# Cross attention: moving the query products and the logits from four PSUM banks to two

## The chip, the cores and the metric

One core of a Trainium2 chip runs the whole program in one launch. The metric is the device time of that launch in microseconds, as the median of several runs; lower is better. PSUM, the memory that matmuls write, has eight banks of 128 x 512 float32 each, and this program hands them out by name: two to a pool called `mm`, four to `ps`, two to `pr`.

## The reference

The program computes two transformer blocks in float32. The first holds a mixer of four branches, a dense feed-forward and a mixture of experts, over two layers. The second holds, in each of two layers, a mixer (an attention mixer in layer 0, gated linear attention in layer 1), a cross attention to 256 memory rows and a feed-forward. Only the cross attention of the second block is touched. With S = 256 tokens, a width of 1024 and 4 heads of 256:

```python
def mem_cross_attention(h, mem_n, w_q, w_kv, q_gain, k_gain, w_out):
    q = rmsnorm((h @ w_q).reshape(Bn, S, X_HEADS, X_HEAD_DIM), q_gain)
    k, v = jnp.split(mem_n @ w_kv, 2, axis=-1)
    k = rmsnorm(k.reshape(Bn, M, X_HEADS, X_HEAD_DIM), k_gain)
    s = jnp.einsum('bqhd,bkhd->bhqk', q, k) * (X_HEAD_DIM ** -0.5)
    p = jax.nn.softmax(s, axis=-1)
    o = jnp.einsum('bhqk,bkhd->bqhd', p, v).reshape(Bn, S, D_MODEL)
    return o @ w_out
```

## The kernel before

Weights come from HBM in chunks of 128 x 1024 float32 (512 KB). `load` (L536) issues the transfer on SyncE's queue, ScalarE copies the chunk to a rounded high part (`wh`, L469) and VectorE subtracts that to give the low part (`wl`, L482). A product with a weight is then three matmuls for each 128 rows of the weight: high by high, low by high and high by low (`lin`, L571). Six pairs of `wh` and `wl` buffers go round; a pair is free for the next chunk when the second of the two token tiles has used it.

A framework sets the order of the instructions on each engine when the program is built: it goes through the recorded operations with a list scheduler that knows priorities, data and buffers, and afterwards each engine runs its own list in that order and waits on semaphores. So a buffer that is free later can move an instruction to another place in the list of any engine. `bank` (L363) is where a PSUM tile is taken: a pool with n buffers gives the same bank again after n tiles, and the new tile waits until the old one has been read.

The cross attention (L1801) works so:

- `rms_split` (L1419) makes the normalized input X as a high and a low part, transposed.
- The query product is four groups of 24 matmuls of 128 x 512, called q0 to q3 here: q0 and q1 are the two token tiles of the first half of the columns (heads 0 and 1), q2 and q3 those of the second half (heads 2 and 3). `lin_tm` (L592) takes one bank for each, from `ps` (the argument on L1809).
- Each group is read by `head_rms` (L1744): ScalarE squares it (two ACTIVATE of 128 x 256 with a sum), VectorE makes the reciprocal root from the sums in a chain of small operations, and two SCALAR_TENSOR_TENSOR (L479, 128 x 256 each) scale the group and its gain into SBUF. That is the last reading of the bank. `to_fm` (L1770) turns the result with four transposes (L385, bank `pr`) and ScalarE copies it out.
- The logits are four groups, L0 to L3, one for a pair of heads and a token tile (hp, t on L1816 and L1817); each is four matmuls of 128 x 256 in one bank of `ps` (L1819), and each of these matmuls shows as two records, float32 being passed twice. L0 needs q0, L1 needs q1, L2 q2 and L3 q3.
- `softmax_pair` (L764) reduces the maximum on VectorE (TENSOR_REDUCE, L768), takes the exponential on ScalarE with its sum (the last reading of the bank), and scales on VectorE. `pT` (L790) turns the result (four transposes, P0 to P3 here, bank `pr`), ScalarE copies it out, and eight matmuls of 128 x 128 (o0 to o3, sixteen records each, bank `pr`) give the output, which `split` (L493) stores in parts.
- `out_proj` (L628) multiplies by the output weight in four accumulators of 128 x 512, all from `ps`, and `residual` (L1365) adds them to x.

Ahead of the cross attention stands the output projection of the mixer, with its four accumulators in `ps` too. The `mm` banks were last used by the projections of the mixer.

Of the kernel before, what the change touches and what calls it, by code (L numbers as in the profile page):

```python
# [21 lines left out]
S = 256  # L22
# [242 lines left out]
class Net:  # L265
# [27 lines left out]
    def T(self, shape, name=None, dt=F32, keep=False):  # L293

        n = 1
        for d in shape[1:]:
            n *= d
        w = n if dt != BF else (n + 1) // 2
        arena = self.arenar if dt == F32R else (self.cur or self.arena)
        ap, key = arena.alloc(w)  # L300
        key = (arena, key)
        own = self.scopes[-1] if self.scopes and not keep else None
        if own is not None:
            own.append(key)
        v = ap[:shape[0], :w]
        if dt not in (F32, F32R):
            v = v.bitcast(dt)
        if len(shape) == 3:
            v = v.rearrange("p (a b) -> p a b", a=shape[1])
        elif len(shape) == 4:  # L310
            v = v.rearrange("p (a b c) -> p a b c", a=shape[1], b=shape[2])
        self.keys[id(v)] = (key, v, own)
        return v
# [1487 lines left out]
    def cross_attention(self, x, l, kv, st, st2):  # L1801
        T = self.T
        kT, vm = kv
        with self.scope():
            g = self.rows(f"xg{l}", 0, 256)
            X, rs = self.rms_split(x, f"norm_mem_q{l}", st)
            qT = T([128, 8, S])
            for b in range(2):
                for t, _, ps in self.lin_tm(X, f"xq{l}", b, ("ps", "ps")):  # L1809
                    with self.scope():  # L1810
                        qn = T([128, 512])
                        self.head_rms(qn, ps, 2, 256, g, rs[t])
                        self.to_fm(qT, t, qn, 4 * b)
            self.free(*X, *rs)
            O = self.newX()
            for hp in range(2):  # L1816
                for t in range(2):  # L1817
                    with self.scope():
                        lg = self.ps([128, 2, S])  # L1819
                        for j in range(2):  # L1820
                            h = 2 * hp + j
                            for k in range(2):
                                self.mmul(lg[:, j], qT[:, 2 * h + k, t * 128:(t + 1) * 128], kT[:, 2 * h + k, :], k == 0,
                                          k == 1)
                        P = self.softmax_pair(lg, S, 0.0625)
                        PT = self.pT(P, S, "pr")
                        o = self.pr([128, 4, 128])
                        for j in range(2):
                            h = 2 * hp + j
                            for m in range(2):  # L1830
                                for k in range(2):
                                    c = h * 256 + m * 128
                                    self.mmul(o[:, 2 * j + m], vm[k][:, c:c + 128], PT[:, 2 * j + k], k == 0, k == 1)
                        sl = (slice(None), slice(4 * hp, 4 * hp + 4), slice(t * 128, (t + 1) * 128))
                        self.split(O[0][sl], O[1][sl], o)
        self.free(kT, *vm)
        for t, b, ps in self.out_proj(O, f"xo{l}"):
            self.residual(x, t, b, ps, st2)
        self.free(*O)
# [304 lines left out]
```

## Time and profile before

| what | us |
| --- | --- |
| median of 3 runs | 2115.01 |
| lowest and highest run | 2112.03, 2117.79 |
| the profiled execution's own time | 2118.59 |
| span of the profile (first to last instruction) | 2116.9 |
| TensorE matmul (PE) busy | 2051.8 (97%) |
| VectorE (DVE) busy | 1495.5 (71%) |
| ScalarE (ACT) busy | 1153.3 (54%) |
| mean granted TensorE clock | 0.989 of full speed |

The times of single instructions come from the profiled execution, which is one run and not the median. The cross attention of layer 0 stands at about 1417 to 1481 us of the span, that of layer 1 at about 1854 to 1918 us. A row of the timeline gives the start, the length from the first start to the last end of a merged group, the engine, the line, the operation and, in brackets, the idle time before it and what ended it.

### The profile page before, as it was taken

What the parts mean: (1) busy time and instruction counts of PE and PEld (TensorE: products, weight loads), DVE (VectorE), ACT (ScalarE), POOL (GpSimd) and SP (SyncE); (2) the same over time, 40 slices, a digit from 0 to 9 for tenths busy, and PEclk for the clock granted to TensorE, in tenths of its full rate; (3) what the DMA queues carried; (4) which work ended last, traced back from release to release, by engine and by line L of the source; (5) the groups of instructions that cost most, each with busy time, mean ns of one, the idle gap of its engine ahead of it and who ended that gap; (6) DMA issues with size and microseconds to landing.
All of it is one profiled execution on the core that took longest, in us unless ns stands there. A gap on an engine that the chain in (4) does not pass through costs nothing. (4 is left out here: it accounts for less than half of the span.)

```text
span 2116.9 us, 31337 instructions
## 1 busy us (share of the span) xinstructions
PE 2051.8 (97%) x11520; PEld 1688.7 (80%) x11520; DVE 1495.5 (71%) x2916; ACT 1153.3 (54%) x1732; POOL 41.4 (2%) x111
## 2 busy tenths in 40 slices
PE   8999989997999999999999998999999999999999
PEld 8878778886986877888888886877888777878887
DVE  6876686546787578988888898976654657676453
ACT  5544544443544454777777785564544455555442
POOL 1000000000000000000000000000000000000000
PEclk9999999998999999999999999999999999999999
DMA  7333656551453455799999985545555353555551
GB/s 240 132 114 111 223 172 197 184 187 68 165 155 98 121 205 170 273 329 329 341 348 330 328 320 193 186 132 192 187 180 184 111 178 118 187 181 172 176 198 60
DMA packets 118259, 411.39 MB, mean 194 GB/s; under 512 B 13584, under 2 KB 13744, under 8 KB 118096
## 3 DMA queue, kind: packets, MB, share of 16 engines
q1 hardware_dynamic: 113184, 392.91, 54.3%
q0 software_dynamic: 4912, 16.39, 2.5%
q8 instruction: 92, 1.51, 0.3%
q14 instruction: 71, 0.58, 0.1%
HBM read 408.20 MB, written 1.05 MB: 193 GB/s over the span
## 5 line engine op out<-in xcount | busy, mean ns | idle before, releaser
L382 PE MATMUL mm<-wh,ar 128*128 128x512 f32 (+3 forms) x3200 | 976.2, 386 | 13.2 <-PEq L1714 4.4
L382 PEld LDWEIGHTS mm<-wh,ar 128*128 128x128 f32 x3200 | 588.3, 190 | 128.7 <-issue 14.2
L482 DVE TENSOR_TENSOR wl<-raw,wh 128x1024 fp32r<-128x1024 f32 (+3 forms) x464 | 548.1, 1193 | 197.0 <-ACT wh L469 186.0
L469 ACT ACTIVATE wh<-raw 128x1024 fp32r<-128x1024 f32 (+3 forms) x464 | 476.3, 1035 | 293.0 <-PE mm L382 173.1
L382 PE MATMUL mm<-wl,ar 128*128 128x512 f32 (+3 forms) x1600 | 613.4, 384 | 1.2 <-DVE wl L482 1.2
L482 DVE TENSOR_TENSOR wl<-af,wh 128x1024 fp32r<-128x1024 f32 (+2 forms) x300 | 347.3, 1173 | 152.3 <-ACT wh L469 138.5
L469 ACT ACTIVATE wh<-af 128x1024 fp32r<-128x1024 f32 (+2 forms) x300 | 303.7, 1020 | 155.6 <-PE mm L382 56.0
L382 PE MATMUL ps<-wh,ar 128*128 128x512 f32 x1104 | 349.2, 394 | 2.2 <-ACT ar L469 2.2
L382 PEld LDWEIGHTS mm<-wl,ar 128*128 128x128 f32 x1600 | 303.2, 189 | 56.3 <-DVE wl L482 2.4
L382 PEld LDWEIGHTS ps<-wh,ar 128*128 128x128 f32 x1104 | 206.2, 188 | 44.7 <-ACT ar L469 3.8
L382 PE MATMUL ps<-wl,ar 128*128 128x512 f32 x552 | 215.4, 390 | 0.0
L382 PE MATMUL mm<-ar,wh 128*128 128x256 f32 x704 | 131.8, 288 | 0.0
L469 ACT ACTIVATE ar<-pr 128x512 fp32r<-128x512 f32 (+1 forms) x124 | 67.0, 549 | 114.1 <-PE pr L385 97.9
L385 PE MATMUL pr<-ident,af 128*128 128x128 f32 x584 | 98.0, 287 | 31.4 <-DVE af L479 19.2
L382 PEld LDWEIGHTS ps<-wl,ar 128*128 128x128 f32 x552 | 103.7, 188 | 20.9
L385 PEld LDWEIGHTS pr<-ident,af 128*128 128x128 f32 x584 | 68.5, 144 | 63.6 <-issue 27.4
L382 PE MATMUL pr<-wh,ar 128*128 128x512 f32 x352 | 111.5, 394 | 1.2 <-ACT ar L469 1.0
L382 PEld LDWEIGHTS mm<-ar,wh 128*128 128x128 f32 x704 | 109.6, 191 | 3.3 <-issue 2.0
L469 ACT ACTIVATE af<-af 128x512 f32<-128x512 f32 (+5 forms) x132 | 63.8, 491 | 66.6 <-DVE af L482 48.4
L382 PE MATMUL mm<-ar,wl 128*128 128x256 f32 x352 | 99.4, 282 | 0.0
L482 DVE TENSOR_TENSOR ar<-pr,ar 128x512 fp32r<-128x512 f32 (+1 forms) x116 | 71.8, 628 | 37.2 <-ACT ar L469 37.1
L382 PE MATMUL pr<-af,af 64*64 64x32 f32 (+8 forms) x1132 | 84.4, 244 | 2.3 <-ACT af L469 2.3
(197 smaller groups left out, 1683.0 us busy)
## 6 DMA issues: line engine op xcount, KB each, us to landing
af<-in_e_dram SPq DMA_DIRECT2D x127, 512.0 KB, 5.2
raw<-in_win_dram SPq DMA_DIRECT2D x108, 512.0 KB, 4.6
raw<-in_e_dram SPq DMA_DIRECT2D x81, 512.0 KB, 5.2
af<-in_gu_dram SPq DMA_DIRECT2D x56, 512.0 KB, 4.2
af<-in_w_dram SPq DMA_DIRECT2D x42, 512.0 KB, 4.3
raw<-in_xkv_dram SPq DMA_DIRECT2D x32, 512.0 KB, 4.4
raw<-in_gu_dram SPq DMA_DIRECT2D x32, 512.0 KB, 4.5
af<-in_e_dram SPq DMA_DIRECT2D x38, 384.0 KB, 4.9
```

What stands on the lines that cost most here:

```text
L382: return self.pe(self.nc.tensor.matmul(out, lhsT=lhsT, rhs=rhs, start=start, stop=stop, skip_group_check=True), lhsT, rhs)
L385: return self.pe(self.nc.tensor.transpose(out, in_, ident), in_, ident, 1)
L469: return self.nc.scalar.activation(out, in_, f, **kw)
L482: return (eng or self.nc.vector).tensor_tensor(out, a, b, op=op)
```

## The change

The query products take their banks from `lin_tm`'s default, which is `mm` for both token tiles, and the logits take theirs from `mm`. So q0 to q3 and L0 to L3 go through two banks in turn, where they went through four. The output projection keeps its four banks of `ps`, and nothing else in the cross attention is in `ps` any more. No instruction is added or removed.

```diff
@@ cross_attention
-                for t, _, ps in self.lin_tm(X, f"xq{l}", b, ("ps", "ps")):
+                for t, _, ps in self.lin_tm(X, f"xq{l}", b):
...
-                        lg = self.ps([128, 2, S])
+                        lg = self.mm([128, 2, S])
```

The lists of the engines change with it, in both layers in the same way. Three places in layer 0 follow. In the names, `ps_15020` or `mm_15020` is the bank of q1, `15081` of q2, `15130` of q3, `15179`, `15208`, `15237` and `15266` of L0 to L3; `pr_15014`, `pr_15063`, `pr_15124` and `pr_15173` are the transposes of q0 to q3, and `pr_15191` those of P0.

TensorE at the end of q1, before:

```order
L382 MATMUL ps_15020<-wl4_85,ar2_76 128x512
L382 MATMUL ps_15081<-wh0_80,ar2_76 128x512
L382 MATMUL ps_15081<-wh0_80,ar3_77 128x512
...
L385 MATMUL pr_15014<-ident_93,af6_67 128x128 x2
L382 MATMUL ps_15081<-wh0_80,ar2_76 128x512
L385 MATMUL pr_15014<-ident_93,af6_67 128x128 x2
L382 MATMUL ps_15081<-wh0_80,ar3_77 128x512
```

and with the change:

```order
L382 MATMUL mm_15020<-wl4_85,ar2_76 128x512
L385 MATMUL pr_15014<-ident_93,af6_67 128x128 x4
L382 MATMUL mm_15081<-wh0_80,ar2_76 128x512
L382 MATMUL mm_15081<-wh0_80,ar3_77 128x512
...
L385 MATMUL pr_15063<-ident_93,af7_68 128x128 x2
L382 MATMUL mm_15081<-wl2_83,ar2_76 128x512
L385 MATMUL pr_15063<-ident_93,af7_68 128x128 x2
```

Twelve matmuls of q2 stood ahead of the transposes of q0; now none does. q2 takes the bank of q0, and 11 matmuls of q2 stand ahead of the transposes of q1, which stood behind the last of q2.

VectorE between the reciprocal root of q2 and its scaling, before:

```order
L482 TENSOR_TENSOR af0_61<-af0_61 128x2 x2
L482 TENSOR_TENSOR wl0_81<-raw0_78,wh0_80 128x1024
L479 SCALAR_TENSOR_TENSOR af0_61<-af0_61 128x2
L474 TENSOR_SCALAR af0_61<-af0_61 128x2
L482 TENSOR_TENSOR wl2_83<-raw1_79,wh2_82 128x1024
L479 SCALAR_TENSOR_TENSOR af10_71<-ps_15081,af0_61,af2_63 128x256 x2
L482 TENSOR_TENSOR wl0_81<-raw1_79,wh0_80 128x1024
L482 TENSOR_TENSOR wl4_85<-raw0_78,wh4_84 128x1024
L476 TENSOR_SCALAR af0_61<-af0_61 128x2 x2
L768 TENSOR_REDUCE af0_61<-ps_15179 128x2
```

and with the change:

```order
L482 TENSOR_TENSOR wl0_81<-raw0_78,wh0_80 128x1024
L479 SCALAR_TENSOR_TENSOR af0_61<-af0_61 128x2
L482 TENSOR_TENSOR af0_61<-af0_61 128x2
L482 TENSOR_TENSOR wl2_83<-raw1_79,wh2_82 128x1024
L482 TENSOR_TENSOR af0_61<-af0_61 128x2
L479 SCALAR_TENSOR_TENSOR af0_61<-af0_61 128x2
L482 TENSOR_TENSOR wl0_81<-raw1_79,wh0_80 128x1024
L474 TENSOR_SCALAR af0_61<-af0_61 128x2
L482 TENSOR_TENSOR wl4_85<-raw0_78,wh4_84 128x1024
L479 SCALAR_TENSOR_TENSOR af10_71<-mm_15081,af0_61,af2_63 128x256 x2
L476 TENSOR_SCALAR af0_61<-af0_61 128x2 x2
```

The scaling of q2 stood behind two low parts of weights of the output projection and now stands behind four. The maxima of the logits (L768), the first three of which stood ahead of the scaling of q3, now stand behind it.

TensorE at the logits, before:

```order
L382 MATMUL ps_15130<-wl4_85,ar2_76 128x512
L382 MATMUL ps_15179<-af5_66,af9_70 128x256
L385 MATMUL pr_15124<-ident_93,af10_71 128x128 x4
L382 MATMUL ps_15179<-af5_66,af9_70 128x256 x3
L382 MATMUL ps_15208<-af5_66,af9_70 128x256 x4
L382 MATMUL ps_15237<-af5_66,af9_70 128x256 x4
L385 MATMUL pr_15173<-ident_93,af10_71 128x128 x4
L385 MATMUL pr_15191<-ident_93,af3_64 128x128 x4
L382 MATMUL ps_15266<-af5_66,af9_70 128x256 x2
```

and with the change:

```order
L382 MATMUL mm_15130<-wl4_85,ar2_76 128x512
L385 MATMUL pr_15124<-ident_93,af10_71 128x128 x4
L382 MATMUL mm_15179<-af5_66,af9_70 128x256 x4
L385 MATMUL pr_15173<-ident_93,af10_71 128x128 x4
L382 MATMUL mm_15208<-af5_66,af9_70 128x256 x4
L382 MATMUL mm_15237<-af5_66,af9_70 128x256 x2
L385 MATMUL pr_15191<-ident_93,af3_64 128x128 x4
L382 MATMUL mm_15237<-af5_66,af9_70 128x256 x2
```

L0, L1 and L2 stood in one run ahead of the transposes of q3; now L0 stands behind the transposes of q2, L1 behind those of q3, and L2 directly after L1, in the bank of L0. On ScalarE the load of the table for the exponential stood ahead of the copies of the transposes of q3 and now stands behind them.

## Rows read from the trace of the kernel before

**Rows 1.** The page: busy time of the engines, shares of the last chain.

```profile
PE 2051.8 (97%) x11520; PEld 1688.7 (80%) x11520; DVE 1495.5 (71%) x2916; ACT 1153.3 (54%) x1732; POOL 41.4 (2%) x111
PE 35%; DVE 3%; DMA 1%; issue 0%; ACT 0%; ACTq 0%; DVEq 0%; SPq 0%
```

**Rows 2.** Timeline of PE, layer 0, from the start of q2 to o3.

```profile
1430.30 0.62 PE L382 MATMUL ps<-wh,ar 128*128 128x512 f32 x2
...
1433.80 0.41 PE L385 MATMUL pr<-ident,af 128*128 128x128 f32 x2 [0.62 <-DVE af L479]
...
1434.29 0.38 PE L385 MATMUL pr<-ident,af 128*128 128x128 f32 x2
1434.42 0.48 PE L382 MATMUL ps<-wh,ar 128*128 128x512 f32 x1
...
1437.23 0.41 PE L385 MATMUL pr<-ident,af 128*128 128x128 f32 x2
...
1443.18 0.59 PE L382 MATMUL ps<-af,af 128*128 128x256 f32 x2
...
1444.16 4.91 PE L382 MATMUL ps<-af,af 128*128 128x256 f32 x22
1450.75 1.50 PE L385 MATMUL pr<-ident,af 128*128 128x128 f32 x8 [1.68 <-DVE af L479]
1452.40 2.07 PE L382 MATMUL ps<-af,af 128*128 128x256 f32 x4
1454.26 2.54 PE L382 MATMUL pr<-af,af 128*128 128x128 f32 x16
...
1457.08 1.03 PE L382 MATMUL ps<-af,af 128*128 128x256 f32 x4
1457.98 2.05 PE L382 MATMUL pr<-af,af 128*128 128x128 f32 x16
1459.86 0.60 PE L385 MATMUL pr<-ident,af 128*128 128x128 f32 x4
...
1464.46 2.02 PE L382 MATMUL pr<-af,af 128*128 128x128 f32 x16
```

**Rows 3.** Timeline of DVE, layer 0.

```profile
1433.18 0.87 DVE L479 SCALAR_TENSOR_TENSOR af<-ps,af,af 128x256 f32<-128x256 f32 x2
1433.97 0.23 DVE L476 TENSOR_SCALAR af<-af 128x2 f32<-128x2 f32 x2
...
1436.60 0.88 DVE L479 SCALAR_TENSOR_TENSOR af<-ps,af,af 128x256 f32<-128x256 f32 x2
1438.27 0.24 DVE L476 TENSOR_SCALAR af<-af 128x2 f32<-128x2 f32 x2 [0.79 <-ACT af L469]
...
1442.96 0.87 DVE L479 SCALAR_TENSOR_TENSOR af<-ps,af,af 128x256 f32<-128x256 f32 x2
1443.75 2.35 DVE L482 TENSOR_TENSOR wl<-raw,wh 128x1024 fp32r<-128x1024 f32 x2
...
1446.15 0.69 DVE L768 TENSOR_REDUCE af<-ps 128x2 f32<-128x512 f32 x1
...
1450.13 0.87 DVE L479 SCALAR_TENSOR_TENSOR af<-ps,af,af 128x256 f32<-128x256 f32 x2
```

**Rows 4.** Timeline of ACT, layer 0.

```profile
1437.21 0.48 ACT L469 ACTIVATE af<-ps,af 128x256 f32<-128x256 f32 x1 [1.91 <-PE ps L382]
...
1443.15 1.06 ACT L469 ACTIVATE wh<-raw 128x1024 fp32r<-128x1024 f32 x1 [0.29 <-PE ps L382]
...
1447.12 1.28 ACT L469 ACT_TABLE_LOAD   x1 [1.51 <-DVE af L476]
```

**Rows 5.** Stretches, layer 0: us, PE, PEld, DVE, ACT, POOL busy, PEclk, DMA, GB/s.

```profile
1452.40:1454.30 1.90, 1.90 (x5) 1.54 (x6) 0.78 (x3) 0.94 (x3) 0.00 (x0) 0.50 0.53 149
1456.60:1460.00 3.40, 3.40 (x28) 3.08 (x28) 1.53 (x3) 1.96 (x6) 0.00 (x0) 1.00 0.26 78
```

**Rows 6.** Timeline of PE, layer 1: the transposes of q3 and P0.

```profile
1887.87 1.70 PE L385 MATMUL pr<-ident,af 128*128 128x128 f32 x8 [1.67 <-DVE af L479]
```

## The prediction

> **What bounds the kernel now.** The page comes first: TensorE (PE) has matmuls in flight for 97% of the span and the chain that ended last is mostly PE [rows 1]. So whatever makes PE stand still longer shows in the time almost one for one, unless a later wait takes it up. The timeline of PE through the cross attention of layer 0 is read next [rows 2]. The reader is to see two stalls there, both at transposes (L385) that wait for VectorE's scaling of a query product (L479): 0.62 us ahead of those of q0 at 1433.80, and 1.68 us ahead of those of q3 at 1450.75. Then VectorE's timeline, to see what stands ahead of these scalings in its list [rows 3], ScalarE's for the squares, the weights and the table load [rows 4], and the granted clock of single stretches [rows 5]. No stretch of PE waits for a bank of `ps` that the output projection would want: its first matmuls stand among the attention outputs, behind all the logits. So I find nothing that the freed banks could give, and ask what the two shared banks and the new lists cost.
>
> **Prices.** L0 to L2 are 24 records of 128x256, with four transposes among them, from 1443.18 to 1444.16 + 4.91 = 1449.07. Four records take 1457.98 - 1457.08 = 0.90, so a logit group of eight takes 1.8, and four transposes 5.89 - 5.40 = 0.5. From 1437.23 to 1443.18 stand the four transposes of q1 and the 24 matmuls of q3: 5.95 - 0.5 = 5.45, or 0.227 a matmul. An attention output takes 1459.86 - 1457.98 = 1.88 [rows 2].
>
> **Step A, the transposes of q0 lose their cover.** Before, 12 matmuls of q2 (from 1430.30) ran while VectorE finished q0. VectorE's list is the same up to the scaling of q0 at 1433.18 [rows 3], and what it waits for is older than q2, so the transposes still start at 1433.80. But with the change nothing may run in between: PE should stand still from about 1430.5 to 1433.8, some 3.2 us. q2 starts at 1434.42, where before its 14th matmul stood: 13 x 0.227 = 2.95 us late. Its 11 matmuls then end at 1436.9; the transposes of q1 still wait for VectorE until 1437.23, with the second pair half a us later, and q2's last 12 matmuls end at 1437.84 + 12 x 0.227 = 1440.6. Before, ScalarE squared q2 at 1437.21 [rows 4], so q2 is 3.4 us late. q3 ends at 1440.6 + 5.45 = 1446.0 against 1443.18: 2.8 us late, the transposes of q1 being done by then.
>
> **Step B, the scaling of q2 falls behind four weights.** VectorE's chain for q2 starts 1438.27 - 1437.21 = 1.06 after its squares start, so at 1441.7. From there to the scaling took 1442.96 - 1438.27 = 4.69 with two low parts in between; now four stand there, two more for 2.35 [rows 3]. That gives 1441.7 + 4.69 + 2.35 = 1448.7. The last of the four high parts follows the end of q3 (at 1443.15 before [rows 4], so about 1446.1 now, done 1447.2), which does not delay this further. The transposes start 0.62 after the scaling, as at q0: 1449.3. PE has nothing in front of them and stands still from 1446.0 to 1449.3, 3.3 us. L0 follows at 1449.9 and ends at 1451.7.
>
> **Step C, q3.** Its chain, now without maxima in it, starts 0.79 after the scaling of q2 (1433.18 to 1433.97 at q0), at 1449.5, and takes what q1's took, 1436.60 - 1433.97 = 2.63 [rows 3]: scaling at 1452.1, where it was at 1450.13. The transposes start at 1452.7, after 1.0 us of idle, and L1 runs from 1453.4 to 1455.2.
>
> **Step D, the bank of L0.** L2 must wait until L0's exponentials have been read out. Its maximum runs at 1452.9 to 1453.6. ScalarE first copies the transposes of q3 (1453.5 to 1454.1), then loads its table, 1.28 us [rows 4], then runs two exponentials at about 0.48, as the squares of this shape: 1456.4. The table load was hidden behind L1 and L2; now it stands between L0 and L2. L2 starts at 1456.5, after 1.3 us of idle.
>
> **From there to o3** PE has L2 and L3 (3.6), the transposes of P0 to P3 (2.0), o0 to o2 (5.6) and eight matmuls of the output projection (1.8), as before in other order: 13.0, less 0.2 for transposes that overlap their neighbours, so o3 starts at 1469.3. It started at 1464.46 [rows 2]: 4.8 us late. Copies, maxima and exponentials of P1 to P3 lie beside this work, as before; were their cover gone, 0.2 to 0.5 at each. After o3 the lists are the same, and PE runs 88 weight matmuls of the output projection whose weights wait for free buffers only; nothing there takes the loss back.
>
> **The clock.** After the stall of 1.68 us the granted clock stood at 0.50, 1.2 GHz, over 1452.4 to 1454.3, and at 1.00, 2.4 GHz, again later [rows 5]. It shows in the rows: four logit records 2.07 against 1.03, an attention output 2.54 against 2.05 [rows 2], 1.04 + 0.49 = 1.5 us together. That is in the 1464.46 above, and the 1469.3 has none of it. Stalls A and B are both longer than 1.68 us, so I expect a stretch at 1.2 GHz after each. After A it falls on q2, whose end everything waits for: 1.5, less 0.3 that the transposes of q1 wait anyway, 1.2. After B it falls on L0 and L1, beside 1.0 us of idle in step C: between 0.5 and 1.5, and I take 0.7, nearer the low end because L0 comes first. Bounds: none of both (0), and 1.5 each with a third one after steps C and D (4.5).
>
> **Sum.** 4.8 + 1.2 + 0.7 = 6.7 us for a layer. Layer 1 has the same lists and the same second stall, 1.67 us at 1887.87 [rows 6], so 13.4 in all. SyncE moves one weight load of the feed-forward past its neighbours in each layer; it is needed long after, and costs nothing. The sum stands against the profiled execution, 2118.59 us, which becomes 2132.0; that run lies 3.6 above the median of the runs shown, so the median to expect is 2115.01 + 13.4 = 2128.4.
>
> **Rivals.** A measurement of this kernel tells about 0.3%, 6.3 us, from no change.
>
> - The clock stays at 2.4 GHz after A and B, or falls only where PE waits anyway: 2 x 4.8 = 9.6, so 2124.6. For it: behind the 0.62 us stall at 1433.80 PE kept its pitch, 11 matmuls from 1434.42 to 1437.23 [rows 2]. Against it: 3.3 is twice the stall after which it fell.
> - A third slow stretch in each layer, since PE now goes through four waits in 26 us: 2 x (4.8 + 4.5) = 18.6, so 2133.6. The Trainium skill, "TensorE: Matmul & The Clock Gate", section "A second HAM failure mode: psum-queue depth-cycling", tells of this: a kernel that cycles through PSUM banks lets PE idle briefly and often, and its clock swings between the two levels. The trace agrees as far as one swing for each layer, at 1452.4 [rows 5]; more of it no row here shows.
> - Only step A counts: the scaling of q2 comes as early relative to q3 as before, and steps B to D hide. 2 x 2.95 = 5.9, so 2120.9, at the edge of what can be told. Against it stands VectorE's list, which lets q2's scaling run only after the last chunk of q3.
> - Faster: VectorE comes out ahead of PE. The maxima of L0 to L2 (0.69 each [rows 3]) no longer delay q3's scaling. It came 1450.13 - 1442.96 = 7.2 after that of q2; without the maxima and the two low parts it needs 0.79 + 2.63 = 3.4. If that relief reached all four scalings, both stalls (0.62 and 1.68) and the 1.5 us of slow clock would go: 2 x 3.8 = 7.6 gained, 2107.4. It decides at where the scalings end: q0's by 1430.5, the end of q1, and q2's by about 1445.5. The list leaves the first at 1434.05 (1433.18 + 0.87), and step B puts the second at 1449.6, four us too late. The Trainium skill, "Perfetto Trace Analysis", section "Matmul Optimizations", is on the side of faster in general: use all eight banks. By that the freed four should let more run side by side; no row here shows PE wait for them.
>
> **Chances.** The forecast with its slow stretches 0.50, the full clock 0.17, the third stretch 0.14, step A alone 0.09, faster 0.05, and 0.05 for losses that later stages take up. Slower by over 0.3%: the first three and half of step A, 0.86; within 0.3%: the other half and the losses taken up, 0.09; faster 0.05. The range reaches from step A alone less the scatter of the median, 2120, to the third stretch with the 2.8 by which the highest run shown exceeds the median, 2137.
>
> **What would show it.** Right: a wait of about 3 us on L479 ahead of the transposes of q0 and another ahead of those of q2, in both layers; L2 waiting for L469; the table load after the copies of q3's transposes; a granted clock of 0.50 near the starts of q2 and of L0; o3 later by 5 to 9 us; and the two cross attentions alone longer. Wrong: q2's scaling before the end of q3, or a feed-forward or mixer whose length changes too.

## The result and the profile after

The changed kernel takes 2129.48 us, the median of six runs (2126.54 to 2132.08). Before took 2114.62 in the same comparison (six runs, 2112.03 to 2119.6). The ratio is 1.0063, with a 95% interval from 1.0052 to 1.0075: slower by 13.3 us, between 11 and 16 (the two medians lie 14.9 apart). The profiled execution has a span of 2128.9 us, 12.0 more than the 2116.9 of before.

The page of the changed kernel, the rows that answer to [rows 1]:

```profile
PE 2055.4 (97%) x11520; PEld 1691.7 (79%) x11520; DVE 1496.6 (70%) x2916; ACT 1153.7 (54%) x1732; POOL 41.2 (2%) x111
PE 36%; DVE 2%; ACT 1%; issue 1%; DMA 0%; ACTq 0%
```

PE has 3.6 us more of work in flight for the same 11520 matmuls (2055.4 against 2051.8), and the rest of the 12 us it stands still. The page tells no more than that. The timeline of PE in layer 0 of the changed kernel, with the rows that answer to [rows 2], tells where:

```profile
1433.40 1.08 PE L385 MATMUL pr<-ident,af 128*128 128x128 f32 x4 [3.25 <-DVE af L479]
1434.14 1.20 PE L382 MATMUL mm<-wh,ar 128*128 128x512 f32 x2
...
1438.98 0.52 PE L385 MATMUL pr<-ident,af 128*128 128x128 f32 x2
...
1442.30 0.39 PE L382 MATMUL mm<-wl,ar 128*128 128x512 f32 x1
...
1451.19 0.74 PE L385 MATMUL pr<-ident,af 128*128 128x128 f32 x4 [3.07 <-DVE af L479]
1451.77 1.89 PE L382 MATMUL mm<-af,af 128*128 128x256 f32 x8
1454.61 0.74 PE L385 MATMUL pr<-ident,af 128*128 128x128 f32 x4 [0.95 <-DVE af L479]
1455.18 1.89 PE L382 MATMUL mm<-af,af 128*128 128x256 f32 x8
1458.37 1.13 PE L382 MATMUL mm<-af,af 128*128 128x256 f32 x4 [1.29 <-ACT af L469]
...
1471.38 1.97 PE L382 MATMUL pr<-af,af 128*128 128x128 f32 x16
```

The reader is to see four stalls where before had two: 3.25 us ahead of the transposes of q0, 3.07 ahead of those of q2, 0.95 ahead of those of q3, 1.29 ahead of L2. The matmul at 1442.30 is the 24th and last of q2. The last row is o3, at 1471.38 against 1464.46.

VectorE in layer 0, the scaling of q0, the first and the last of the four low parts, and the scalings of q2 and of q3, as in [rows 3]:

```profile
1432.78 0.87 DVE L479 SCALAR_TENSOR_TENSOR af<-mm,af,af 128x256 f32<-128x256 f32 x2
...
1445.28 1.23 DVE L482 TENSOR_TENSOR wl<-raw,wh 128x1024 fp32r<-128x1024 f32 x1
...
1449.43 1.22 DVE L482 TENSOR_TENSOR wl<-raw,wh 128x1024 fp32r<-128x1024 f32 x1
1450.57 0.87 DVE L479 SCALAR_TENSOR_TENSOR af<-mm,af,af 128x256 f32<-128x256 f32 x2
...
1453.98 0.88 DVE L479 SCALAR_TENSOR_TENSOR af<-mm,af,af 128x256 f32<-128x256 f32 x2
```

ScalarE in layer 0, the table load, as in [rows 4], now with the first exponential of L0 behind it:

```profile
1456.00 1.28 ACT L469 ACT_TABLE_LOAD   x1
1457.30 0.47 ACT L469 ACTIVATE af<-mm,af 128x256 f32<-128x256 f32 x1
```

PE in layer 1 of the changed kernel: the transposes of q0, those of q2, L0, the transposes of q3, L1, the first half of L2, and o3:

```profile
1877.65 0.74 PE L385 MATMUL pr<-ident,af 128*128 128x128 f32 x4 [3.12 <-DVE af L479]
...
1893.13 1.02 PE L385 MATMUL pr<-ident,af 128*128 128x128 f32 x4 [3.06 <-DVE af L479]
1893.94 3.23 PE L382 MATMUL mm<-af,af 128*128 128x256 f32 x8
1897.00 0.60 PE L385 MATMUL pr<-ident,af 128*128 128x128 f32 x4
1897.44 1.89 PE L382 MATMUL mm<-af,af 128*128 128x256 f32 x8
1900.62 1.13 PE L382 MATMUL mm<-af,af 128*128 128x256 f32 x4 [1.29 <-ACT af L469]
...
1913.62 1.98 PE L382 MATMUL pr<-af,af 128*128 128x128 f32 x16
```

Here L0 took 3.23 us, where it took 1.89 in layer 0, and the stall ahead of the transposes of q3 is gone. Stretches of the changed kernel, in the columns of [rows 5]: the first two are behind the stalls at q0 and at q2 in layer 0, the last two the same in layer 1.

```profile
1434.20:1439.10 4.90, 4.90 (x14) 3.73 (x13) 2.51 (x12) 0.60 (x1) 0.00 (x0) 0.50 0.44 166
...
1451.60:1455.00 3.40, 2.45 (x14) 1.79 (x14) 2.98 (x15) 0.60 (x1) 0.00 (x0) 1.00 0.80 288
1877.70:1890.00 12.30, 12.24 (x56) 9.57 (x56) 7.20 (x32) 5.53 (x10) 0.00 (x0) 1.00 0.44 141
1893.30:1896.60 3.30, 3.30 (x11) 2.66 (x11) 2.88 (x17) 0.60 (x1) 0.00 (x0) 0.50 0.92 336
```

So the clock fell to 1.2 GHz once in each layer: at the first stall in layer 0 (6.8 us in all, from 1432.4, a microsecond before that stall ends), behind the second in layer 1 (3.4 us).

**One measure for all runs.** A kernel's span also holds what the clock did far away from the change. So the runs below are compared over two sections of PE's list: from the same matmul of the mixer's output projection to the same matmul of the feed-forward behind it, found by counting PE's matmuls (in before they start at 1400.22 and 1490.07, and at 1845.01 and 1930.05). The stretch between the two sections takes 354.94 us before and 355.29 after, the one behind them 182.36 and 182.33: the loss lies in the sections alone. "Slow" is how long the granted clock stood at 0.50 within them, and the last column takes that off at 1.5 us for each 3.4 us, the price worked out in the prediction from [rows 2]. That price is an estimate for other stretches. "Idle" is the length of the two sections less the time that PE is busy in them; it needs no price, though slow matmuls can fill a wait.

| kernel | layer 0 | layer 1 | sum | idle | slow | sum without slow |
| --- | --- | --- | --- | --- | --- | --- |
| before | 89.86 | 85.03 | 174.9 | 8.5 | 6.8 | 171.9 |
| before, second profile | 90.47 | 84.88 | 175.4 | 8.7 | 6.8 | 172.4 |
| the change | 97.02 | 89.92 | 186.9 | 19.3 | 10.2 | 182.4 |
| the change, second profile | 96.45 | 89.99 | 186.4 | 19.8 | 6.8 | 183.4 |
| query products alone in `mm` | 91.88 | 88.24 | 180.1 | 14.5 | 3.4 | 178.6 |
| logits alone in `mm` | 88.33 | 83.42 | 171.8 | 8.7 | 0 | 171.8 |
| q2, q3 and logits in `mm` | 92.70 | 88.13 | 180.8 | 12.1 | 13.6 | 174.8 |
| six banks | 88.58 | 82.97 | 171.6 | 8.2 | 0 | 171.6 |
| the change, low parts held | 96.39 | 89.91 | 186.3 | 18.5 | 10.2 | 181.8 |
| before, low parts held | 88.79 | 85.49 | 174.3 | 8.7 | 3.4 | 172.8 |
| logits in `mm`, table early | 88.98 | 84.08 | 173.1 | 9.8 | 0 | 173.1 |
| logits in `mm`, low parts held | 88.66 | 83.54 | 172.2 | 8.9 | 0 | 172.2 |
| logits in `mm`, both | 88.86 | 83.95 | 172.8 | 9.5 | 0 | 172.8 |

PE's busy time bears the price out. In the five kernels with no slow stretch in either layer it is 84.0 to 84.2 us in the section of layer 0 and 79.1 to 79.3 in that of layer 1. Where a section has slow stretches, it is 1.3 to 2.0 us longer for each 3.4 us of them.

### The profile page after: what moved, and what is told of

Same layout as the page of the kernel before. It is cut to its first block, busy times and chain, and to the rows that moved or that the text cites. A ratio compares the mean times of both kernels' runs of the same rounds, so it can differ in the third digit from the quotient of the medians.

```text
span 2128.9 us, 31337 instructions
## 1 busy us (share of the span) xinstructions
PE 2055.4 (97%) x11520; PEld 1691.7 (79%) x11520; DVE 1496.6 (70%) x2916; ACT 1153.7 (54%) x1732; POOL 41.2 (2%) x111
## 3 DMA queue, kind: packets, MB, share of 16 engines
HBM read 408.20 MB, written 1.05 MB: 192 GB/s over the span
## 5 line engine op out<-in xcount | busy, mean ns | idle before, releaser
L382 PE MATMUL mm<-wh,ar 128*128 128x512 f32 (+3 forms) x3328 | 1021.1, 388 | 13.0 <-PEq L1714 4.6
L382 PEld LDWEIGHTS mm<-wh,ar 128*128 128x128 f32 x3328 | 614.9, 191 | 134.1 <-issue 14.7
L382 PE MATMUL mm<-wl,ar 128*128 128x512 f32 (+3 forms) x1664 | 640.2, 385 | 0.2 <-DVE wl L482 0.2
L382 PEld LDWEIGHTS mm<-wl,ar 128*128 128x128 f32 x1664 | 316.4, 190 | 57.9 <-DVE wl L482 1.2
L382 PE MATMUL ps<-wh,ar 128*128 128x512 f32 x976 | 307.3, 393 | 1.1 <-ACT ar L469 1.1
L382 PEld LDWEIGHTS ps<-wh,ar 128*128 128x128 f32 x976 | 182.2, 188 | 38.5 <-ACT ar L469 2.1
L382 PE MATMUL ps<-wl,ar 128*128 128x512 f32 x488 | 190.5, 390 | 0.0
L382 PEld LDWEIGHTS ps<-wl,ar 128*128 128x128 f32 x488 | 91.7, 188 | 18.6
L469 ACT ACTIVATE af<-mm,af 128x512 f32<-128x512 f32 (+1 forms) x86 | 50.7, 591 | 102.6 <-PE mm L382 98.8
```

Of the source, the lines that this page charges most:

```text
L382: return self.pe(self.nc.tensor.matmul(out, lhsT=lhsT, rhs=rhs, start=start, stop=stop, skip_group_check=True), lhsT, rhs)
L469: return self.nc.scalar.activation(out, in_, f, **kw)
```

## The experiments

The theory from the prediction: step A comes from q2 wanting the bank of q0, step B from the four low parts ahead of q2's scaling, step D from L2 wanting the bank of L0. Rivals: the logits make the loss, the clock makes it, or leaving `ps` costs by itself.

### One half of the change at a time, and six banks

**Query products alone.**

```diff
-                for t, _, ps in self.lin_tm(X, f"xq{l}", b, ("ps", "ps")):
+                for t, _, ps in self.lin_tm(X, f"xq{l}", b):
```

> Before, with the query products alone in mm; the logits keep ps. Theory (two banks in turn for q0 to q3 make PE wait for the scaling of q0 and push the scaling of q2 behind four low parts): step A whole, a wait of about 3.2 us on L479 ahead of the transposes of q0 in both layers. Step B half hidden: the scaling of q2 still comes behind four low parts, at about 1449 in layer 0, but PE has L0 and part of L1 to do before its transposes. Steps C and D not as with the change, since L2 needn't wait for L0's bank, but the maxima stand ahead of the scaling of q3 again. So 3 to 5.5 us a layer, 2121 to 2126 for a before of 2114.6. Rival (the logits' two banks and the table load make the loss): within 2 us of before. Rival (the clock makes most of it): only as much as the stretches at a granted clock of 0.50 grow, 1.5 us for each 3.4 us of it.

Measured: 2124.63 us, ratio 1.0039 (1.0026 to 1.0052), 8.3 us slower. PE in layer 0, at the transposes of q0, at L0 and L1, at the transposes of q2 and of q3:

```profile
1432.88 0.74 PE L385 MATMUL pr<-ident,af 128*128 128x128 f32 x4 [3.26 <-DVE af L479]
...
1445.13 2.75 PE L382 MATMUL ps<-af,af 128*128 128x256 f32 x12
1448.37 0.41 PE L385 MATMUL pr<-ident,af 128*128 128x128 f32 x2 [0.48 <-DVE af L479]
...
1453.42 1.48 PE L385 MATMUL pr<-ident,af 128*128 128x128 f32 x8 [1.32 <-DVE af L479]
```

Step A is there whole, and it is more than half of the loss: 6.7 of the 10.5 us that the last column gives for the change, or 6.0 of 10.8 by the idle time. VectorE's list has the same four low parts ahead of q2's scaling as with the change, yet PE waits 0.48 us for it and not 3.07: L0 and half of L1 run in front, the 12 records of the second row. That the logits alone make the loss is refuted.

**Logits alone.**

```diff
-                        lg = self.ps([128, 2, S])
+                        lg = self.mm([128, 2, S])
```

> Before, with the logits alone in mm; the query products keep ps. Theory: the transposes of q0 keep the 12 matmuls of q2 in front of them, and the scaling of q2 stands behind two low parts as before, so steps A and B are gone; only L2's wait for the exponentials of L0 is left (step D, 1.3 us at most, as much as the change showed), and one maximum less stands ahead of the scaling of q3 (0.7 us won). 0 to 1.5 us a layer, 2114 to 2118 for a before of 2114.6. Rival (the logits make the loss): 5 us a layer or more, 2125 or above, with an idle of 3 us or more at L2.

Measured: 2113.67 us, ratio 0.9987 (0.9977 to 0.9997), so 2.8 us faster if anything. PE in layer 0 at L2:

```profile
1449.24 1.13 PE L382 MATMUL mm<-af,af 128*128 128x256 f32 x4 [2.14 <-ACT af L469]
```

L2 waits for the bank of L0, longer than with the change, but the stall of 1.68 us ahead of the transposes of q3 [rows 2] is gone in exchange: by the time L2 has run, q3 is scaled. The two cancel (171.8 and 171.9 without slow stretches, 8.7 and 8.5 us idle). What was won is that the clock stayed at 1.00 behind the 2.14 us, so 175.4 or 174.9 became 171.8.

**Six banks, none still to be read when it is taken.**

```diff
-                for t, _, ps in self.lin_tm(X, f"xq{l}", b, ("ps", "ps")):
+                for t, _, ps in self.lin_tm(X, f"xq{l}", b, (("mm", "mm"), ("ps", "ps"))[b]):
...
-                        lg = self.ps([128, 2, S])
+                        lg = self.bank(("ps", "mm")[hp], [128, 2, S])
```

> Before, with mm used beside ps: q0 and q1 in mm, q2 and q3 in ps, L0 and L1 in ps, L2 and L3 in mm, so no bank of q0 is wanted by q2 and none of L0 by L2. Theory (what costs is that q2 and L2 take a bank that must first be read out, not which pool a group lies in): 12 matmuls of q2 stand ahead of the transposes of q0 and two low parts ahead of the scaling of q2, as before, so 2112 to 2117 for a before of 2114.6. Rival (leaving ps for mm costs by itself, by a wait for the mixer's last use of mm or for the bank that the output projection takes next): 2118 or more, with a wait at q0, L2 or the first matmul of the output projection.

Measured: 2116.06 us, ratio 0.9996 (0.9985 to 1.0007). PE in layer 0, at the transposes of q0 and of q3:

```profile
1432.76 0.41 PE L385 MATMUL pr<-ident,af 128*128 128x128 f32 x2 [1.05 <-DVE af L479]
...
1449.50 1.48 PE L385 MATMUL pr<-ident,af 128*128 128x128 f32 x8 [1.67 <-DVE af L479]
```

The two waits are those of before (0.62 and 1.68), and there is none ahead of the transposes of q2. Using `mm` costs nothing that can be told; taking a bank that is still to be read does. Nor do two more banks win anything that can be told. The Trainium skill, "Perfetto Trace Analysis", section "Matmul Optimizations", advises using all eight banks; with the two of `pr` this kernel does, and its ratio shows no gain from that alone.

### Step B: the low parts, or the banks of q2 and q3

If the four low parts make step B, then holding them back must undo it. `hold` lets the weight preparation of the output projection go past its first two low parts only when the named instruction has been placed, here the last scaling.

```diff
-                        self.stt(v(out)[:, h], v(src)[:, h], r[:, h:h + 1], gain, OP.mult, OP.mult)
+                        self.scaled = self.stt(v(out)[:, h], v(src)[:, h], r[:, h:h + 1], gain, OP.mult, OP.mult)
...
+        self.hold = (self.scaled, 2)
         for t, b, ps in self.out_proj(O, f"xo{l}"):
```

**With the change.**

> The change, with the low parts of the output projection's weights past the first two held back until the scaling of q3 has been issued, so that no low part stands between the scalings of q1, q2 and q3. Theory: step A stays (3.2 us ahead of the transposes of q0), step B is gone, since the transposes of q2 then run inside the matmuls of q3 with 17 of them in front; steps C and D are left or smaller. The loss of the change falls from 14.9 to what step A makes with its slow stretch, 2.9 to 4.5 us a layer, less the old stall of 1.68 us ahead of the transposes of q3 if that goes too: 2117 to 2124. The low parts now come later; if the output projection waits for them, that shows as a new wait of L382 on L482 ahead of its first matmuls. Rival (step B's stall is made by something else than the low parts): the time of the change, 2129. Rival (the sum of VectorE's work decides, the place doesn't): 2129 too.

Measured: 2128.15 us, ratio 1.0058 (1.0041 to 1.0075): the time of the change, though the edit did what it should. PE in layer 0, at the transposes of q2, at L0 and at the transposes of q3:

```profile
1442.16 0.41 PE L385 MATMUL pr<-ident,af 128*128 128x128 f32 x2 [0.58 <-DVE af L479]
...
1444.26 1.89 PE L382 MATMUL mm<-af,af 128*128 128x256 f32 x8
1450.02 0.41 PE L385 MATMUL pr<-ident,af 128*128 128x128 f32 x2 [3.88 <-DVE af L479]
```

The transposes of q2 do run inside q3 now, and the stall has moved to those of q3. VectorE between the scalings of q2 and of q3 shows no low part that could be blamed, only waiting for q3's squares and its own chain:

```profile
1441.53 0.87 DVE L479 SCALAR_TENSOR_TENSOR af<-mm,af,af 128x256 f32<-128x256 f32 x2
1446.22 0.24 DVE L476 TENSOR_SCALAR af<-af 128x2 f32<-128x2 f32 x2 [3.82 <-ACT af L469]
...
1449.39 0.88 DVE L479 SCALAR_TENSOR_TENSOR af<-mm,af,af 128x256 f32<-128x256 f32 x2
```

So the expectation fell, and step B's reason with it. The new theory: L0 takes the bank of q2 and L1 that of q3, so neither can run before that group has been scaled. Before, L0, L1 and L2 stood in front of the last transposes; now one logit group does, wherever VectorE's list puts the low parts.

**q2, q3 and the logits in `mm`, q0 and q1 in `ps`.** This leaves step A out, has two low parts ahead of q2's scaling as before, and keeps only L0 and L1 in the banks of q2 and q3.

```diff
-                for t, _, ps in self.lin_tm(X, f"xq{l}", b, ("ps", "ps")):
+                for t, _, ps in self.lin_tm(X, f"xq{l}", b, (("ps", "ps"), ("mm", "mm"))[b]):
...
-                        lg = self.ps([128, 2, S])
+                        lg = self.mm([128, 2, S])
```

> Before, with q0 and q1 left in ps, q2 and q3 in mm, and all logits in mm: so q2 doesn't wait for the bank of q0, but L0 and L1 take the banks of q2 and q3, as with the change. Theory, as the runs so far leave it (steps B and C are made by L0 and L1 waiting for the banks of q2 and q3, so that nothing is left to run in front of these transposes; how many low parts VectorE does first only sets where the wait stands): no wait before the transposes of q0 beyond the 0.6 us of before, then 0.5 us before those of q2, L0, and 3 to 4 us before those of q3, where L1 and L2 were the cover. 2.5 to 4.5 us a layer, 2120 to 2124 for a before of 2115.5. Rival (step B is made by the four low parts alone, which are two here as before): 2118 or less. Rival (only step A counts): within 2 us of before.

Measured: 2120.71 us, ratio 1.0013 (1.0004 to 1.0022), 2.8 us slower than its before of 2117.54. PE in layer 0, at the transposes of q2, at L0 and at the transposes of q3:

```profile
1439.51 0.74 PE L385 MATMUL pr<-ident,af 128*128 128x128 f32 x4 [0.28 <-DVE af L479]
1440.09 1.89 PE L382 MATMUL mm<-af,af 128*128 128x256 f32 x8
1445.74 1.94 PE L385 MATMUL pr<-ident,af 128*128 128x128 f32 x8 [3.76 <-DVE af L479]
```

The stall is where the new theory puts it. The idle time ahead of the transposes of q2 and of q3 together is 3.07 + 0.95 = 4.0 with the change (four low parts first), 0.58 + 3.88 = 4.5 with none, 0.28 + 3.76 = 4.0 here with two; with the logits in other banks it is 0.48 + 1.32 = 1.8, with six banks 1.67 and, before, 1.68. The low parts choose the place and the banks set the sum. The time is less than expected: 1.4 us a layer by the ratio and (174.8 - 171.9) / 2 = 1.5 by the sections, where 2.5 to 4.5 stood. L1 and L2, 3.6 us, do stand behind the stall, but with one maximum ahead of it instead of three, q3's scaling comes sooner after that of q0 (1445.11 - 1429.31 = 15.8 against 16.95 in [rows 3]), 1.15 of the 3.6. Of the other microsecond, part is the price of this profile's 13.6 us of slow clock: by idle time the loss is (12.1 - 8.5) / 2 = 1.8 a layer. The rest, some 0.6, is not explained.

The two halves nearly add up: 6.7 for the query products and 2.9 here make 9.6, against 10.5 (182.4 - 171.9) for the change, 11.0 by the second profiles; by idle time 6.0 and 3.6 make 9.6, against 10.8. What is left over both layers, 0.9 to 1.4, is less than L2's wait for L0 in the change, 1.29 in each layer, which neither half has. (With the query products alone L2 waits 0.25 us, but for ScalarE's copy of the transposes of q2.)

### Three attempts at something faster

**Before, low parts held**, with the same edit as above.

> Before, with the low parts of the output projection's weights past the first two held until the scaling of q3, as in the run with the change. Theory (with four banks L0 to L2 need no bank that q2 or q3 still holds, so low parts taken out of the way bring q3's scaling forward and the cover stays): the transposes of q2 run inside the matmuls of q3, L0 to L2 stand behind q3, and the stall of 1.68 us ahead of the transposes of q3 falls to 0.3 to 0.6: 2 x 1.2 us of stall and the stretches at 0.50 that followed it, 2112.5 to 2115 for a before of 2117. The same hold won 1 us or nothing with the change, where L1 waits for q3's bank. Rival (VectorE's chain for q3, not the low parts, sets q3's scaling): within 1 us of before, and the stall stays over 1.3 us.

Measured: 2117.35 us, ratio 1.0008 (0.9998 to 1.0019). No gain. PE in layer 0, at the transposes of q3 and at L3:

```profile
1448.92 0.74 PE L385 MATMUL pr<-ident,af 128*128 128x128 f32 x4 [0.91 <-DVE af L479]
1450.35 0.70 PE L382 MATMUL ps<-af,af 128*128 128x256 f32 x2 [0.69 <-ACT af L469]
```

The stall of 1.68 became 0.91 + 0.69 = 1.6: L3 now waits for ScalarE's copy of the transposes, beside which the transposes of P0 ran before.

**Logits in `mm`, the table loaded early.** The edit beside that of the logits alone follows; `hold` is not used. The result of the added exponential is used nowhere.

```diff
             qT = T([128, 8, S])
+            warm = T([128, 1])
+            self.act(warm, rs[0], AF.Exp)
```

> The logits alone in mm, and an exponential of one column of the query's norm (its result unused) ahead of the query products, so that ScalarE loads its table for exponentials there and not between the last square and the exponentials of L0. Theory (L2 waits 2.1 us for the exponentials of L0, 1.28 of which is the table load): the load is gone from there, L2 waits about 0.9, and the transposes of q3 then wait for VectorE, so 0.5 to 1 us a layer is won against the logits alone in mm: 2112 to 2113.5 where those give 2113.7 to 2114. Rival (the table load lies beside VectorE's maximum and costs nothing): no difference, and L2 waits as long.

Measured: 2115.0 us, ratio 0.999 (0.9979 to 1.0001): no gain over the logits alone. PE in layer 0, at the first matmul of q0 and at L2, and ScalarE shortly before the former:

```profile
1418.47 0.49 PE L382 MATMUL ps<-wh,ar 128*128 128x512 f32 x1 [1.60 <-ACT ar L469]
...
1448.48 1.99 PE L382 MATMUL mm<-af,af 128*128 128x256 f32 x8 [0.86 <-ACT af L469]
```

```profile
1415.82 1.28 ACT L469 ACT_TABLE_LOAD   x1
```

L2 waits 2.14 - 0.86 = 1.28 us less, exactly the load. But the load now stands ahead of the copies that q0 needs, and PE waits 1.60 there where the logits alone show 0.58.

**Logits in `mm`, low parts held**, and the same **with the table early**:

> The logits alone in mm, and the low parts of the output projection's weights past the first two held until the scaling of q3. Theory (the maximum of L0, and with it L2's bank, and the scaling of q3 stand behind four low parts of 1.2 us each): the maximum of L0 comes right behind L0, L2 waits about 0.9 to 1.2 instead of 2.1, the scaling of q3 comes about 1.4 us earlier: 1 to 1.5 us a layer won against the logits alone in mm, 2110.5 to 2112. Rival (the low parts then come too late for the output projection): a new wait of L382 on L482 among its first matmuls, as long as what was won or longer, 2114 or more.

> Both together: the logits alone in mm, the low parts held until the scaling of q3, and the table for exponentials loaded ahead of the query products. Theory: L2 waits for nothing, the transposes of q3 come at most 0.5 us late, and no stretch at a granted clock of 0.50 follows: 1.7 us of stall and up to 1.5 us of slow clock a layer go against before, 2109 to 2112 for a before of 2115.5. Rival (VectorE's sum of work between q2 and o0 is the bound, whatever its order): as before, 2114 to 2116, with the same idle time at a later place.

Measured: 2113.39 us, ratio 0.9982 (0.9973 to 0.9991), and 2113.99 us, ratio 0.9988 (0.9979 to 0.9998), both slower than expected. In the first L2 still waits 1.84 us. In the second it waits 0.56, and the start of q0 pays 1.6 us again. All three kernels with the logits in `mm` and something added have longer sections than the one without. The best ratio, 0.9982, beats both kernels, by 3.8 us against before; that is below the 0.3% that a measurement of this kernel tells from no change, and its sections don't show that the hold is what does it.

### The clock: the same two kernels again

Each was profiled a second time, unchanged.

> The kernel before, unchanged, for a second profile: where does the granted clock stand at 0.50? Theory one (a stall of a given length is followed by a stretch at 0.50 or not depending on when it falls, which varies from one execution to the next, since the six banks' kernel kept 1.00 behind the same stall of 1.67 us): the stalls of 0.6 and 1.68 us stand where they stood, and the stretches at 1452.1 and 1889.0, of 3.4 us each, are missing in at least one layer or have another length; the section from 1400 to 1490 us is then 1.5 us shorter. Theory two (the stall of 1.68 us always brings the stretch in this kernel): both stretches again, each within 1 us of its stall's end as before.

> The changed kernel, unchanged, for a second profile. Theory one (which stall brings a stretch at 0.50, and how long it is, varies): stalls of 3.2, 3.1, 0.95 and 1.3 us again in both layers to within 0.1, but the stretches (6.8 us behind the first stall of layer 0, 3.4 us behind the second of layer 1) in at least one layer at another stall or of another length. Theory two (the lists fix them): the same two stretches. Without any stretch the section of a layer would be 10.5 us longer in sum over both layers than before without any; each 3.4 us at 0.50 adds 1.5.

Measured: 2119.18 and 2125.52 us, one run each. Before has both stretches again, from 1452.9 and 1889.8, 3.4 us each, behind the same stalls of 1.68 us; its waits at q0 are 1.07 and 0.44 us where they were 0.62 and 0.86, so these vary by some half a microsecond in an unchanged kernel. The change has its stalls again to within 0.1, but for the first of layer 0, 3.68; the stretches stand behind the same stalls as in the first profile, 3.4 us from 1430.6 and 3.4 from 1888.0, so the one in layer 0 is half as long. Within the sections the first theory, that the place varies between executions of one kernel, found no support in two profiles; only a length varied. Far from the change the place does vary: before has a granted clock of 0.50 from 626.3 to 629.3 and from 783.3 to 786.3 in its first profile and of 1.00 there in its second, and the reverse from 115.2 to 118.0. So two profiles are too few to say that the lists fix it.

## Why the prediction was right, and where its steps were wrong

The time (2129.48 for 2128.4) and the sign came out, and most of the waits did. One reason did not.

- **What bounds it**: right. PE is the bound, and the loss lies in the two cross attentions alone. No wait for a bank of `ps` was there to win, as the six banks show.
- **Step A**: right in place, size and cause. 3.25 and 3.12 us for "some 3.2"; six banks, where q2 doesn't want the bank of q0, have 1.05 and 0.41 us there (0.62 and 0.86 before), and the query products alone 3.26 and 3.29.
- **Step B**: right in size (3.07 and 3.06 for 3.3), wrong in cause. The prediction put the wait down to the two more low parts in VectorE's list. Without any low part there the wait moved to q3 and the time stayed; with four, but the logits in other banks, it was 0.48. The size came out because the low parts do stand ahead of q2's scaling in this list; they set where the wait stands and not how much of it there is. The prediction's "PE has nothing in front of them" was the real cause, and it did not ask why: L0 needs only q0, yet takes the bank of q2. It had the fact, that L0 now stands behind the transposes of q2, and read it as order where it was a wait.
- **Step C**: 0.95 for 1.0 in layer 0, none in layer 1, where slow matmuls of L0 filled it. It belongs with step B: L1 waits for the bank of q3.
- **Step D**: 1.29 for 1.3 in both layers, the table load on the path as told. Alone, without A to C, this wait is 2.14 and costs nothing, since it replaces the old stall ahead of the transposes of q3. Its worth was read rightly only for this combination.
- **The clock**: the term that was mis-sized. The prediction had a slow stretch after A and one after B in each layer, 1.2 and 0.7 us. There was one in each layer, as there had been before. In layer 0 it lay on q2 for 6.8 us: by the prediction's own sum q2 should end at 1440.6, less the 0.4 by which layer 0 now runs earlier (1432.78 against 1433.18), and it ended at 1442.30 + 0.227, so the clock cost some 2.3 there and not 1.2. In layer 1 it lay on L0: 3.23 - 1.89 = 1.34, less the 0.95 that step C no longer waits, 0.4.
- **The sum**: 4.8 and these make 4.8 + 2.3 = 7.1 and 4.8 + 0.4 = 5.2, beside 7.2 (97.02 - 89.86) and 4.9 (89.92 - 85.03) measured. Predicted were 6.7 and 6.7. The clock came to 2.3 + 0.4 = 2.7 where 3.8 stood, which is most of what lies between the predicted 13.4 and the 12.05 of the sections; the ratio of the runs gives 13.3. That the sum came so near is in part luck: one layer lost more than told and the other less, the slow stretches did not lie as told, and by the second profiles the layers lost 96.45 - 90.47 = 6.0 and 89.99 - 84.88 = 5.1.
- **The rivals**: the clock at full speed fell, as each layer of both profiles has a slow stretch, though in layer 1 most of it fell where PE would have waited anyway. The third stretch fell too: four waits in 26 us gave one stretch in layer 0, as the one wait of 1.68 us had before. The Trainium skill, "TensorE: Matmul & The Clock Gate", section "A second HAM failure mode: psum-queue depth-cycling", tells of a clock that swings between its levels when a kernel cycles through PSUM banks; the trace shows no more swings here than before. "Only step A" is half true: 6.7 of 10.5. "Faster" needed VectorE's relief to reach the scalings; low parts taken wholly out of the way gave nothing, with two banks or four.

What a stall costs in clock remains open. The price of 1.5 us for each 3.4 us slow held, but which stall is followed by a slow stretch, and for how long, was seen and not explained.

## What to carry to other kernels

Before moving groups to fewer banks, write down for each group whose bank it takes and when that bank has been read for the last time: a group that has all its data but takes the bank of a later one in the chain can no longer serve as cover. An instruction list shows such a wait only as an order, so ask of every group that changed its place which bank it waits for, and don't stop at what the other engine has ahead of it. A wait that looks costly (2.14 us at L2) may cost nothing where it stands in place of another one, so measure half of a change before blaming it.

## What the runs showed of the hardware

The clock did not follow the length of the stall. With the query products alone, both layers have the same stall at the transposes of q0 (3.26 and 3.29 us); stretches of that kernel, in the columns of [rows 5], the first behind the stall of layer 0, the second behind that of layer 1:

```profile
1433.00:1436.20 3.20, 3.14 (x15) 2.21 (x14) 2.79 (x17) 0.60 (x1) 0.00 (x0) 1.00 0.93 321
...
1871.50:1874.70 3.20, 3.20 (x9) 2.45 (x9) 2.12 (x10) 0.10 (x1) 0.00 (x0) 0.50 0.67 224
```

With six banks the stall ahead of the transposes of q3 is 1.67 us in both layers, as before, and none is followed by a slow stretch. Stretches of that kernel behind the stall, layer 0 and layer 1:

```profile
1452.90:1456.30 3.40, 3.40 (x28) 3.08 (x27) 1.55 (x4) 1.08 (x2) 0.00 (x0) 1.00 0.00 0
...
1888.00:1892.00 4.00, 4.00 (x33) 3.67 (x32) 1.53 (x3) 1.92 (x6) 0.00 (x0) 1.00 0.40 133
```

And a slow stretch can be twice as long: 6.8 us in both layers with q2, q3 and the logits in `mm`, where it starts at 1444.5, still within the stall of 3.76 us that ends at 1445.74. With the change and the low parts held, layer 0 has two of 3.4 us, from 1430.8 and from 1451.3, behind stalls of 3.24 and 3.88 us, and layer 1 has one.
